# Feed-forward blocks of 384, 384, 384 and 448 columns instead of four of 400, pool weights prepared earlier, sample caches loaded later

## The chip, the core and the metric

The kernel runs on one core of a Trainium2 chip. The metric is device time in microseconds of one execution of the whole program, median of repeated runs. TensorE (PE) multiplies matrices, VectorE (DVE), ScalarE (ACT) and GpSimd (POOL) do the elementwise work, and every transfer is issued by SyncE (SP), whose queue is taken in order.

## The reference, cut to what matters

One layer of a hybrid decoder is applied to a prompt of 2048 tokens and to 8 samples of 8 tokens (64 more columns), all with the same weights, in fp32:

```
h = rmsnorm(x);  proj = h @ w_in                 # 1024 -> 1280: q, k, v and u
attn_o = window attention (128, sinks, ALiBi); samples use cache_win_k, cache_win_v
pool_o = (causal mean over 2, 4, 8, 16 of u - u) @ w_pool * pool_scale; samples use state_pool
x = x + concat(attn_o, pool_o) @ w_out
x = x + cross attention into 256 memory tokens   # samples have their own memory caches
x = x + square(relu(rmsnorm(x) @ w_up)) @ w_down # hidden 4096
y = rmsnorm(x)
```

The outputs are y for both groups and the new window, pool and memory caches.

## The kernel before, in words

Activations lie transposed, features on the 128 partitions and tokens along the free axis. Every fp32 product is made of three fp32r matmuls: an operand is split into a rounded high part and the remainder (`rnd`, and L143 on ACT with L144 on DVE for weights), and high x high, high x low and low x high are added in PSUM (`mm3`, L122 to L124; `dense`, L291 to L293). A weight pair (high, low) is 128x1024 and serves 24 matmuls of a token block.

The prologue computes the memory keys and values, folds them with `w_cq` and `w_co` into matrices that it writes to DRAM (`a_s`, `b_s`), and then three superblocks of two token blocks each follow. The first has 256 and 256 prompt columns, the second block also the 64 sample columns; the other two have 384 and 384. Each superblock goes through the input projection (`in`), attention and pooling (mixed with the rest of the projection), the output projection (`wo`), cross attention, the product with `b_s`, and the feed-forward stage (`up`, `down`): 8 groups of 4 up chunks of 24 matmuls and 4 down pairs of 24 matmuls for each block, so 8 x 4 x 24 + 8 x 4 x 24 = 1536 matmuls per block. In the first superblock the feed-forward runs 512 prompt columns at once. The 64 sample columns leave it before the feed-forward (`xs_s` in DRAM) and ride along in later superblocks: 16 in each of the four blocks, hence 400 columns (`NY`, `NM`).

The weight stream (`Stream`) loads a weight through a staging tile `f` (6 of them), splits it into two of 12 `w` tiles, and runs as many weights ahead as free `w` tiles allow. Small temporaries are `t` tiles (8). The instructions are put on the engines by a scheduler that may move an instruction ahead of others that it does not depend on, but each engine, and SP's queue, runs its list in order.

The pool weights are folded into `w_out`: `prep_fold` loads `cst` and `wpool` and scales `wpool` into a high and low part (L354 on ACT, L355 on DVE), and `fold(g)` multiplies it with the four `wop` weights, between the first chunks of the first superblock's input projection; `put_fold` (L342) copies each result on ACT and writes it to `wo_s`. The loads for the sample part are: `ckz` (1 MB, L534, into the x tile of the second block), `cvz` (two times 512 KB, L522, each in a staging tile `f` until `attn_sample` has ended), `spool`.

Of the kernel before, what the change touches and what calls it, by code (L numbers as in the profile page):

```python
# [9 lines left out]
F32 = mybir.dt.float32  # L10
F32R = mybir.dt.float32r
# [3 lines left out]
P = 128  # L15
# [41 lines left out]
def kernel(ctx: ExitStack, tc: tile.TileContext, io, nW=12, nF=6, nT=8):  # L57
# [13 lines left out]
    FS = Slots([sb(f"f{i}", 1088) for i in range(nF)])  # L71
    ftag = {id(t): f"f{i}" for i, t in enumerate(FS.free)}
    keep = list(FS.free)
    TS = Slots([sb(f"t{i}", 400) for i in range(nT)])
    XT = [sb(f"x{i}", 8 * NM) for i in range(2)]
# [296 lines left out]
    def prologue():  # L372
# [117 lines left out]
    def load_x(bl):  # L490
        src = io["x"][:, 8 * bl.ox:8 * (bl.ox + bl.n)]
        if bl.s == 0:
            nc.sync.dma_start(bl.xt[:, 0:8 * bl.n], src)
        else:
            nc.sync.dma_start(bl.xv[:, :, 0:bl.n], src.rearrange("p (k n) -> p k n", n=bl.n))
            j = 2 * (bl.s - 1) + bl.b
            nc.sync.dma_start(bl.xv[:, :, bl.n:NM], xs_s[:].rearrange("p (k n) -> p k n", n=64)[:, :, 16 * j:16 * j + 16])

    def superblock(s, blks, nxt):
# [15 lines left out]
        if smp:  # L515
            us = X0[:, 4 * uw:4 * uw + 736].rearrange("p (g b t) -> p g b t", g=4, t=23)
            nc.sync.dma_start(X0[:, 4 * uw:4 * uw + 736].rearrange("p (x t) -> p x t", t=23)[:, :, 0:15], io["spool"].rearrange("p (x t) -> p x t", t=15))
            ckz = X1[:, 0:2048].rearrange("p (b v s) -> p b v s", b=8, v=2)
            qz = [X1[:, 2048 + 544 * i:2048 + 544 * (i + 1)] for i in range(2)]
            cvs = [FS.get(), FS.get()]  # L520
            for i in range(2):
                nc.sync.dma_start(cvs[i][:, 0:1024], io["cvz"][:, 1024 * i:1024 * (i + 1)])  # L522
            cvz = [c[:, 0:1024].rearrange("p (b v s) -> p b v s", b=4, v=2) for c in cvs]
            smt = TS.get()
            kS = smt[:, 0:128].rearrange("p (v t) -> p v t", t=64)
            vS = smt[:, 128:384].rearrange("p (v t) -> p v t", t=P)
            nc.gpsimd.memset(smt[:, 0:384], 0.0)
            qf = TS.get()

        def in_evac(c, b, ps):  # L530
            bl = blks[b]
            n = bl.n
            if smp and (c, b) == (0, 0):
                nc.sync.dma_start(X1[:, 0:2048], io["ckz"])  # L534
                nc.gpsimd.memset(X1[:, 2048:3136], 0.0)
            if c == 0:
# [17 lines left out]
                if smp is bl:  # L554
# [207 lines left out]
        def attn_sample():  # L762
            bl = smp
            LS = FS.get()
# [91 lines left out]
        if s == 0:  # L856
            wpr = prep_fold()
        while len(qdone) < len(lead):
# [3 lines left out]
            if s == 0 and m < 4:  # L862
                fold(m, wpr)
# [126 lines left out]
        def sample_cross():  # L990
# [54 lines left out]
            for bg in range(2):  # L1045
                nc.gpsimd.memset(ptz[bg][:, 0:1088], 0.0)
                for mb in range(2):
                    ps = AUX.get()
                    nc.tensor.transpose(ps[:, 0:P], pp[:, 256 * bg + P * mb:256 * bg + P * mb + P], ident[:])
                    for b in range(4):  # L1050
                        nc.vector.tensor_copy(
                            ptz[bg][:, 544 * mb + P * b:544 * mb + P * b + P].rearrange("p (h n) -> p h n", n=32)[:, :, 8 * b:8 * b + 8],
# [5 lines left out]
            for bg in range(2):  # L1058
                for b in range(4):
                    for mb in range(2):  # L1060
                        vv = FS.get()
                        nc.sync.dma_start(vv[:, 0:1024], io["cmv"][4 * bg + b, mb])
                        for h in range(4):
                            nc.tensor.matmul(o2[32 * h:32 * h + 32, 256 * bg:256 * bg + 256],
                                             ptz[bg][:, 544 * mb + P * b + 32 * h:544 * mb + P * b + 32 * h + 32],
# [56 lines left out]
        def after_co(b):  # L1122
# [10 lines left out]
            else:  # L1133
                ml.take += [(GH[b], GH[b].get()) for _ in range(4)]
                if b == 0:
                    ml.f = FS.get()
                    ml.ft = ftag[id(ml.f)]
                    ml.fx = pool.tile([P, 1088], F32R, name=f"{ml.ft}r{s}", tag=ml.ft)
                u = [BIG[f"h{b}"][:, NM * i:NM * i + NM] for i in range(15)] + [ml.fx[:, NM * b:NM * b + NM]]
                ml.h3b[b] = u  # L1140
# [3 lines left out]
        merged = s == 0  # L1144

# [25 lines left out]
        else:  # L1171
            cx = [pool.tile([P, 512], F32R, name=f"cp{b}r{s}", tag=f"cp{b}") for b in range(2)]
            hb = [[BIG[f"q{b}"][:, NM * i:NM * i + NM] for i in range(15)] + [cx[b][:, 0:NM]] for b in range(2)]
            hidu = lambda b, g, i: hb[b][8 * (g % 2) + i]
# [94 lines left out]
        if not merged:  # L1269
            FS.ids.discard(id(ml.f))  # L1270
            f = pool.tile([P, 1088], F32, name=f"{ml.ft}f{s}", tag=ml.ft)
            ftag[id(f)] = ml.ft
            keep.append(f)
            FS.ids.add(id(f))
            FS.put(f)
# [8 lines left out]
    vcarry = [None]  # L1284
    blk = [make_blks(s) for s in range(3)]
# [134 lines left out]
```

## Time and profile before

| what | us |
|---|---|
| median of 3 runs (lowest, highest) | 2657.72 (2656.19, 2660.29) |
| the profiled execution | 2660.15 |
| its span, first to last instruction | 2658.3 |
| PE busy | 2576.7 (97%) |
| DVE, ACT, POOL busy | 1298.3, 974.8, 658.9 |
| prologue | 0 to about 117 |
| input projection of the first superblock up to its sample attention | about 117 to 177 |
| feed-forward of the three superblocks | about 467 to 830, 1168 to 1745, 2074 to 2646 |

The span is what the trace covers; the time of the execution holds 1.85 us more. PE's busy share is not its speed: what counts is the distance between the starts of matmuls and the stretches in which PE waits. The second half of a clock column, PEclk, tells the share of full speed that PE was granted.

### The profile page before, as it was taken

To read this page: it belongs to the slowest core of one execution; us is meant where nothing else is said; L and a number is where in the kernel's file an instruction comes from. 1 tells how busy PE (TensorE), PEld (TensorE's weight loads), DVE (VectorE), ACT (ScalarE), POOL (GpSimd) and SP (SyncE) were. 2 spreads that over 40 slices of the span, in tenths; PEclk is the share of its full clock that TensorE was granted. 3 is DMA by queue.
4 is the path that set the end of the run, shared out by engine and by line. 5 is a ranking of instruction groups with operands and counts; after the bars stand their busy time and mean duration, and the time that the engine had idled before them with its cause. 6 is when DMAs were issued, how large, how long until landed. Compare 5 with 4: busy or idle time off the path is not lost.

```text
span 2658.3 us, 36411 instructions
## 1 busy us (share of the span) xinstructions
PE 2576.7 (97%) x14409; PEld 2407.6 (91%) x14409; DVE 1298.3 (49%) x2256; ACT 974.8 (37%) x1867; POOL 658.9 (25%) x695
## 2 busy tenths in 40 slices
PE   8789999999999999999999999999999999999998
PEld 8688858888879998899999999999979999999997
DVE  7547634644447856353333333689363633333333
ACT  6536424422334744333222222358243422222221
POOL 1205312311125343142111111525332411111111
PEclk9989999999999999999999999999999999999999
DMA  8842266223233041212111111222211111111101
GB/s 275 265 149 89 104 238 237 79 93 104 95 102 128 25 145 33 74 45 72 64 56 64 56 64 56 81 107 81 97 48 64 56 64 64 56 64 56 64 24 50
DMA packets 101823, 245.10 MB, mean 92 GB/s; under 512 B 21972, under 2 KB 41876, under 8 KB 101012
## 3 DMA queue, kind: packets, MB, share of 16 engines
q1 hardware_dynamic: 101652, 242.78, 26.9%
q8 instruction: 113, 1.85, 0.3%
q14 instruction: 58, 0.48, 0.1%
HBM read 219.79 MB, written 22.95 MB: 91 GB/s over the span
## 4 chain that ended last, share of the span: by engine, by line
PE 80%; DVE 8%; ACT 4%; POOL 3%; DMA 3%; issue 2%; SPq 0%; DVEq 0%; ACTq 0%; POOLq 0%
PE mm L124 13%; PE mm L122 13%; PE mm L123 13%; PE mm L292 13%; PE mm L293 12%; PE mm L291 12%; DVE t L243 3%; DVE w L144 1%; POOL t L217 1%; ACT w L143 1%; PE aux L699 1%; DVE acth L246 1%; POOL t L617 1%; ACT x L711 1%; PE aux L730 1%
## 5 line engine op out<-in xcount | busy, mean ns | idle before, releaser
L143 ACT CAST w<-f 128x1024 fp32r<-128x1024 f32 x311 | 325.9, 1050 | 693.3 <-PE mm L123 470.0
L144 DVE TENSOR_TENSOR w<-f,w 128x1024 fp32r<-128x1024 f32 x311 | 393.3, 1269 | 302.8 <-ACT w L143 298.4
L291 PE MATMUL mm<-acth,w 128*128 128x400 f32 (+3 forms) x1568 | 532.6, 340 | 6.6 <-ACT w L143 5.9
L293 PE MATMUL mm<-acth,w 128*128 128x400 f32 (+3 forms) x1568 | 529.4, 338 | 1.2 <-DVE w L144 1.2
L292 PE MATMUL mm<-acth,w 128*128 128x400 f32 (+3 forms) x1440 | 486.8, 338 | 6.1 <-DVE acth L246 5.4
L122 PE MATMUL mm<-actq,w 128*128 128x400 f32 (+2 forms) x1376 | 478.2, 348 | 1.1 <-ACT f L342 1.1
L124 PE MATMUL mm<-actq,w 128*128 128x400 f32 (+2 forms) x1376 | 478.7, 348 | 0.0
L123 PE MATMUL mm<-actq,w 128*128 128x400 f32 (+2 forms) x1248 | 433.5, 347 | 0.0
L1178 POOL TENSOR_TENSOR t<-t 128x400 f32<-128x400 f32 (+1 forms) x136 | 163.1, 1200 | 812.3 <-ACT t L1177 812.3
L291 PEld LDWEIGHTS mm<-acth,w 128*128 128x128 f32 x1568 | 298.1, 190 | 10.1 <-ACT w L143 6.8
L293 PEld LDWEIGHTS mm<-acth,w 128*128 128x128 f32 x1568 | 299.2, 191 | 1.7 <-DVE w L144 1.7
L1239 DVE TENSOR_TENSOR x<-mm,x 128x400 f32<-128x400 f32 (+1 forms) x272 | 152.9, 564 | 281.6 <-PE mm L124 278.6
L292 PEld LDWEIGHTS mm<-acth,w 128*128 128x128 f32 x1440 | 273.9, 190 | 11.2 <-DVE acth L246 7.3
L217 POOL TENSOR_TENSOR t<-t,t 128x384 f32<-128x384 f32 (+3 forms) x161 | 191.2, 1188 | 351.7 <-ACT t L216 348.3
L122 PEld LDWEIGHTS mm<-actq,w 128*128 128x128 f32 x1376 | 259.5, 189 | 11.7 <-ACT f L342 1.5
L124 PEld LDWEIGHTS mm<-actq,w 128*128 128x128 f32 x1376 | 260.8, 190 | 9.5
L291 PE MATMUL mm<-actq,w 128*128 128x384 f32 (+2 forms) x768 | 248.0, 323 | 0.8 <-DVE x L915 0.6
L293 PE MATMUL mm<-actq,w 128*128 128x384 f32 (+2 forms) x768 | 246.2, 321 | 2.0 <-DVE w L144 2.0
L292 PE MATMUL mm<-actq,w 128*128 128x384 f32 (+2 forms) x768 | 246.5, 321 | 0.0
L123 PEld LDWEIGHTS mm<-actq,w 128*128 128x128 f32 x1248 | 235.4, 189 | 9.9
L1180 DVE TENSOR_TENSOR actq<-t,actq 128x400 fp32r<-128x400 f32 (+1 forms) x120 | 71.1, 593 | 222.1 <-ACT actq L1179 222.0
L291 PEld LDWEIGHTS mm<-actq,w 128*128 128x128 f32 x768 | 145.6, 190 | 3.3 <-DVE x L915 0.9
(246 smaller groups left out, 3745.3 us busy)
## 6 DMA issues: line engine op xcount, KB each, us to landing
f<-in_wup SPq DMA_DIRECT2D x89, 512.0 KB, 3.2
f<-in_wdn SPq DMA_DIRECT2D x89, 512.0 KB, 3.2
f<-in_win SPq DMA_DIRECT2D x29, 512.0 KB, 3.2
f<-a_s SPq DMA_DIRECT2D x23, 512.0 KB, 3.8
f<-b_s SPq DMA_DIRECT2D x23, 512.0 KB, 4.2
f<-in_wco SPq DMA_DIRECT2D x16, 512.0 KB, 4.9
f<-in_cmk SPq DMA_DIRECT2D x16, 512.0 KB, 4.2
f<-in_cmv SPq DMA_DIRECT2D x16, 512.0 KB, 5.1
```

Of the source, the lines that this page charges most:

```text
L122: nc.tensor.matmul(ps, Wh(k), Hh(k), start=first and i == 0, stop=False)
L123: nc.tensor.matmul(ps, Wh(k), Hl(k), start=False, stop=False)
L124: nc.tensor.matmul(ps, Wl(k), Hh(k), start=False, stop=final and i == last)
L143: nc.scalar.copy(th[:], r[:, 0:1024])
L144: eng.tensor_tensor(tl[:], r[:, 0:1024], f32(th[:]), ALU.subtract)
L217: self.add.tensor_tensor(self.acc[:, 0:n], self.acc[:, 0:n], t[:, 0:n], ALU.add)
L243: nc.vector.scalar_tensor_tensor(t[:, 0:n], self.x(k), vec[:, g + k:g + k + 1], self.r[:, 0:n], ALU.mult, ALU.mult)
L291: nc.tensor.matmul(ps[:, 0:n], w8(th)[:, k, :], hi(b, k), start=k == 0, stop=False)
L292: nc.tensor.matmul(ps[:, 0:n], w8(th)[:, k, :], lo(b, k), start=False, stop=False)
L293: nc.tensor.matmul(ps[:, 0:n], w8(tl)[:, k, :], hi(b, k), start=False, stop=k == 7)
L1178: nc.gpsimd.tensor_tensor(q, r, r, ALU.mult)
L1239: nc.vector.tensor_tensor(bl.x(m), ps[:, 0:n], bl.x(m), ALU.add)
```

## The change

1. **Widths.** All 64 sample columns ride in the last block: `NX` and `NY` become 384, 384, 384 for the first three blocks of superblocks two and three, and 448 for the last. A block of 384 columns finds its 16 operands in its own activation tiles (`units`); the block of 448 columns fits 13 there and takes 3 (of the up stage) from two staging tiles `f`, and 1 plus 2 (of the down stage) from `f` and `cp` tiles. So superblock two holds back no `f` tile in its feed-forward (one before), and superblock three two (one before). The x loads of the blocks without sample columns become one contiguous run per partition, and the four loads of 16 columns from `xs_s` become one of 64.
2. **Tiles.** `t` tiles are 448 columns wide and 7 instead of 8; `f` tiles 1024 instead of 1088.
3. **Pool weights.** `prep_fold` is called in the prologue, at the fourth chunk of the fold with `w_cq`, instead of at the input projection.
4. **Sample caches.** In program order `ckz` is loaded at chunk 2 of the input projection instead of chunk 0, `cvz` and `spool` at chunk 4 instead of ahead of the projection, and the copy of the old window keys to `out_wks` is issued in `attn_sample`.

```diff
-OFFY = [0, 256, 512, 912, 1312, 1712]
-NX = [256, 320, 400, 400, 400, 400]
-NY = [256, 256, 400, 400, 400, 400]
-NM = 400
+OFFY = [0, 256, 512, 896, 1280, 1664]
+NX = [256, 320, 384, 384, 384, 448]
+NY = [256, 256, 384, 384, 384, 448]
...
-def tile_hybrid_step_kernel(ctx: ExitStack, tc: tile.TileContext, io, nW=12, nF=6, nT=8):
+def tile_hybrid_step_kernel(ctx: ExitStack, tc: tile.TileContext, io, nW=12, nF=6, nT=7):
...
-    FS = Slots([sb(f"f{i}", 1088) for i in range(nF)])
+    FS = Slots([sb(f"f{i}", 1024) for i in range(nF)])
...
-    TS = Slots([sb(f"t{i}", 400) for i in range(nT)])
+    TS = Slots([sb(f"t{i}", 448) for i in range(nT)])
...
         for c in range(8):
+            if c == 3:
+                wpr.append(prep_fold())
             th, tl = S.next(("cq", c))
...
-            j = 2 * (bl.s - 1) + bl.b
-            nc.sync.dma_start(bl.xv[:, :, bl.n:NM], xs_s[:].rearrange("p (k n) -> p k n", n=64)[:, :, 16 * j:16 * j + 16])
+            if bl.nx > bl.n:
+                nc.sync.dma_start(bl.xv[:, :, bl.n:bl.nx], xs_s[:].rearrange("p (k n) -> p k n", n=64))
...
-            if smp and (c, b) == (0, 0):
+            if smp and (c, b) == (2, 0):
                 nc.sync.dma_start(X1[:, 0:2048], io["ckz"])
                 nc.gpsimd.memset(X1[:, 2048:3136], 0.0)
+            if smp and (c, b) == (4, 1):
+                for i in range(2):
+                    cvs.append(FS.get())
+                    nc.sync.dma_start(cvs[i][:, 0:1024], io["cvz"][:, 1024 * i:1024 * (i + 1)])
+                    cvz.append(cvs[i][:, 0:1024].rearrange("p (b v s) -> p b v s", b=4, v=2))
+                nc.sync.dma_start(X0[:, 4 * uw:4 * uw + 736].rearrange("p (x t) -> p x t", t=23)[:, :, 0:15], io["spool"].rearrange("p (x t) -> p x t", t=15))
...
-                        nc.sync.dma_start(io["wks"][r, :, 0:120], ckz[r, :, kv, 8:P])
...
-        if s == 0:
-            wpr = prep_fold()
...
-                fold(m, wpr)
+                fold(m, wpr[0])
...
-                if b == 0:
-                    ml.f = FS.get()
-                u = [BIG[f"h{b}"][:, NM * i:NM * i + NM] for i in range(15)] + [ml.fx[:, NM * b:NM * b + NM]]
+                if bl.ny > NB:
+                    ml.f = [FS.get() for _ in range(2)]
+                    ml.ex = [x[:, bl.ny * i:bl.ny * i + bl.ny] for x in ml.fx for i in range(2)]
+                ml.h3b[b] = u = units("h", bl, 0, 3)
...
+        def units(g, bl, a, z, more=()):
+            n = bl.ny
+            u = [BIG[f"{g}{bl.b}"][:, n * i:n * i + n] for i in range(16 * NB // n)]
+            if n > NB:
+                u += ml.ex[a:z] + list(more)
+            return u
```

The lists of the engines move at three places. The first is SP's queue behind the last group of `b_s` writes, where the input projection begins (`win` and `wop` are weights, `wo_s` the folded results). Before:

```order
L522 DMA f_82<-in_cvz 128x1024
L522 DMA f_81<-in_cvz 128x1024
L351 DMA f_83<-in_wpool 128x512
L561 DMA out_wks<-x_94 512x1x120
L557 DMA out_wks<-t_92 1024x1x8
L561 DMA out_wks<-x_94 512x1x120
L344 DMA wo_s<-f_84 128x4x128
L344 DMA wo_s<-f_79 128x4x128
L142 DMA f_83<-in_win 128x1024
L142 DMA f_84<-in_wop 128x1024
```

In the changed kernel:

```order
L530 DMA x_93<-in_ckz 128x2048
L342 DMA wo_s<-f_82 128x4x128
L342 DMA wo_s<-f_83 128x4x128
L140 DMA f_84<-in_win 128x1024
L140 DMA f_79<-in_wop 128x1024
L559 DMA out_wks<-t_89 1024x1x8
L342 DMA wo_s<-f_80 128x4x128
L342 DMA wo_s<-f_82 128x4x128
L140 DMA f_83<-in_wop 128x1024
L140 DMA f_80<-in_win 128x1024
L140 DMA f_82<-in_win 128x1024
L767 DMA out_wks<-x_93 512x1x120
```

`cvz` and `wpool` are gone from here, `ckz` has come (before, it stood 24 rows further up, ahead of the last `a_s` write), and the second `win` weight still stands behind the two `wo_s` writes of the first fold.

The second place is SP's queue where the fold with `w_cq` writes its first results (`a_s`). In the changed kernel, with `wpool` ahead of the first `a_s` write and the last `wcqt` weight behind the fifth, where it stood ahead of the first:

```order
L398 DMA out_mv<-t_86 128x256
L349 DMA f_84<-in_wpool 128x512
L342 DMA a_s<-f_82 128x512
L342 DMA a_s<-f_83 128x512
L342 DMA a_s<-f_79 128x512
L342 DMA a_s<-f_80 128x512
L342 DMA a_s<-f_82 128x512
L140 DMA f_79<-in_wcqt 128x1024
```

The third is PE's list after the first chunk of the input projection. Before, the second block's part of that chunk (128x320) came first and the fold (128x512) after all of it:

```order
L292 MATMUL mm_98<-acth_64,w_71 128x320
L293 MATMUL mm_98<-acth_64,w_72 128x320
L122 MATMUL mm_96<-w_73,w_69 128x512
L123 MATMUL mm_96<-w_74,w_69 128x512
L124 MATMUL mm_96<-w_73,w_69 128x512
L122 MATMUL mm_97<-w_73,w_69 128x512
```

In the changed kernel the first fold stands ahead of the second block's part:

```order
L290 MATMUL mm_94<-acth_63,w_73 128x256
L291 MATMUL mm_94<-acth_63,w_74 128x256
L120 MATMUL mm_95<-w_75,w_77 128x512
L120 MATMUL mm_96<-w_75,w_77 128x512
L289 MATMUL mm_97<-acth_64,w_73 128x320
L121 MATMUL mm_95<-w_76,w_77 128x512
```

The fold has moved by one chunk of 24 matmuls on PE. The lines of the changed kernel have numbers lower by 2 here: the copy L342 is L340, its write L344 is L342, `dense`'s L291 to L293 are L289 to L291.

More of the change, by code (lines that the diff above doesn't have):

```diff
@@ L56, with kernel @@
 @with_exitstack
[L57 removed]
+def kernel(ctx: ExitStack, tc: tile.TileContext, io, nW=12, nF=6, nT=7):
     nc = tc.nc
@@ L763, in attn_sample @@
             bl = smp
+            for kv in range(2):
+                r = slice(64 * kv, 64 * kv + 64)
+                nc.sync.dma_start(io["wks"][r, :, 0:120], ckz[r, :, kv, 8:P])
             LS = FS.get()
@@ L1171, in superblock, with hidb @@
         else:
-            cx = [pool.tile([P, 512], F32R, name=f"cp{b}r{s}", tag=f"cp{b}") for b in range(2)]
-            hb = [[BIG[f"q{b}"][:, NM * i:NM * i + NM] for i in range(15)] + [cx[b][:, 0:NM]] for b in range(2)]
-            hidu = lambda b, g, i: hb[b][8 * (g % 2) + i]
+            hb = {}
+            def hidb(b):
+                if b not in hb:
+                    more = []
+                    if blks[b].ny > NB:
+                        more = [pool.tile([P, 512], F32R, name=f"cp{i}r", tag=f"cp{i}")[:, 0:blks[b].ny] for i in range(2)]
+                    hb[b] = units("q", blks[b], 3, 4, more)
+                return hb[b]
+            hidu = lambda b, g, i: hidb(b)[8 * (g % 2) + i]
         def relu2(ps, hi, lo, n, r, q):
```

28 lines of the change are left out of this document (8 added, 20 removed).

## The prediction

> **What bounds the kernel now.** I read the engines' shares and the chain of waits first.
>
> ```profile
> PE 2576.7 (97%) x14409; PEld 2407.6 (91%) x14409; DVE 1298.3 (49%) x2256; ACT 974.8 (37%) x1867; POOL 658.9 (25%) x695
> PE 80%; DVE 8%; ACT 4%; POOL 3%; DMA 3%; issue 2%; SPq 0%; DVEq 0%; ACTq 0%; POOLq 0%
> ```
>
> PE sets the end nearly everywhere, so two things can move the time: the distance between matmul starts in the long stages, and the stretches in which PE waits or runs slowly. For the first, matmuls counted in stretches of one width, two of feed-forward and one of the prologue (window, PE busy and count, weight loads, DVE, ACT, POOL, then PEclk and DMA), and DVE's adds behind groups of 24 matmuls at 384 columns, two groups apart:
>
> ```profile
> 1300.00:1700.00 400.00, 400.00 (x2196) 399.73 (x2195) 145.46 (x200) 102.76 (x160) 74.00 (x65) 1.00 0.19 64
> 30.00:58.00 28.00, 28.00 (x234) 27.95 (x233) 23.87 (x37) 16.55 (x29) 7.81 (x9) 1.00 0.89 299
> 500.00:760.00 260.00, 260.00 (x1149) 215.36 (x1148) 111.52 (x169) 77.31 (x96) 38.16 (x24) 1.00 0.28 98
> ...
> 2057.07 0.56 DVE L1119 TENSOR_TENSOR x<-mm,x 128x384 f32<-128x384 f32 x1 [3.60 <-PE mm L293]
> 2065.39 0.56 DVE L1119 TENSOR_TENSOR x<-mm,x 128x384 f32<-128x384 f32 x1 [3.60 <-PE mm L293]
> ```
>
> At 400 columns a matmul starts every 400.00 / 2196 = 0.1821 us; at 512 columns (first superblock) every 260.00 / 1149 = 0.2263; at 256 (prologue) every 28.00 / 234 = 0.1197; at 384 every 8.32 / 48 = 0.1733. PE never waits there, at full clock. The line through 384 and 512 has 0.0530 / 128 = 0.00041 us per column; at 256 it gives 0.1208, near the 0.1197, at 400 it gives 0.1799. So 400 columns lie 2.2 ns above the line.
>
> For the second, the place where PE loses most, the start of the first input projection:
>
> ```profile
> 100.00:120.00 20.00, 17.68 (x81) 14.24 (x81) 5.82 (x5) 11.69 (x18) 0.00 (x0) 0.91 0.97 299
> 120.00:140.00 20.00, 8.71 (x36) 6.95 (x34) 6.27 (x15) 7.30 (x17) 1.60 (x6) 0.74 0.76 215
> 140.00:160.00 20.00, 16.31 (x79) 14.87 (x80) 7.61 (x10) 8.16 (x11) 0.00 (x0) 0.76 0.72 219
> ...
> L291 PE MATMUL mm<-acth,w 128*128 128x320 f32 x21 | 7.1, 337 | 1.8 <-ACT w L143 1.8
> L291 PE MATMUL mm<-acth,w 128*128 128x256 f32 x10 | 4.3, 432 | 4.1 <-ACT w L143 4.1
> L122 PE MATMUL mm<-w,w 128*128 128x512 f32 x8 | 4.2, 531 | 7.9 <-ACT w L354 7.9
> ```
>
> The last three rows are the groups of 120 to 160 us with the wait ahead of each behind the second bar. L292 and L293 go with L291, L123 and L124 with L122, so PE ran 63 matmuls of 320 columns, 30 of 256 and 24 of 512. By the line these take 63 x 0.147 + 30 x 0.121 + 24 x 0.226 = 18.3 us, and 40 went by: 21.7 lost. Waits are 7.9 + 4.1 + 1.8 = 13.8 of it; most of the rest is the clock, granted at 0.74 and 0.76. The chain of waits, in order of time, tells what was late:
>
> ```profile
> 115.61 6.28 DMA f<-in_wop
> 121.91 1.06 ACT w L143
> 123.00 1.24 DVE w L144
> 124.69 6.12 DMA f<-in_wpool
> 135.45 4.17 DMA f<-in_win
> 139.65 1.05 ACT w L143
> ```
>
> The pool weights were issued at 124.69, behind 1 MB of `cvz`; the fold waited for them. The next `win` weight was issued at 135.45 only, since it stands behind the fold's two writes on SP.
>
> **Feed-forward widths.** Nothing is added or removed: 1536 matmuls per block before and after, 1600 columns in four blocks. Before, four blocks cost 4 x 0.1821 = 0.7284 us per matmul of each. After, 3 x 0.1733 plus a matmul of 448 columns, which the trace does not have. Bounds: on the line, 0.1733 + 64 x 0.00041 = 0.1998; with twice the 2.2 ns that 400 columns lie above it, 0.2042. I take the line: 256, 384 and 512 columns all start their operands at multiples of 256 bytes and lie on it, and operands of 448 columns (1792 bytes) do so too, where those of 400 columns (1600 bytes) do not; that this is the cause is my inference. The gain is (0.7284 - 0.5199 - 0.1998) x 1536 = **13.4**, with the other bound 6.6.
>
> The elementwise work of a 448-column chunk stays hidden: one up chunk takes PE 24 x 0.1998 = 4.8 us, and its slowest step is POOL's square,
>
> ```profile
> L1178 POOL TENSOR_TENSOR t<-t 128x400 f32<-128x400 f32 (+1 forms) x136 | 163.1, 1200 | 812.3 <-ACT t L1177 812.3
> SPq L142 <- DVE w L144: 1800.3, 246, 30.9
> ```
>
> 1.2 us at 400, 1.35 at 448. With seven `t` tiles three chunks of two are in flight, 14 us of PE time; uncovered, a wait of 1.2 us on each of 128 chunks would cost 154. In the last superblock the weight stream has four staging tiles instead of five; the second row (waits of SP: total, times, longest) says that SP already waits for staging tiles, but up to five finished weight pairs stand ahead of PE, 8.7 us each. I cost both at 0.
>
> The Trainium skill, "TensorE: Matmul & The Clock Gate", section "Back-to-back issue gap", gives the isolated gap as N/2.4 + 2.5 ns: 169.2 at 400, 162.5 at 384. By it the four blocks need the same time before and after, and the term would be 0, since it knows only a sum of columns. The rows differ from it by 10.8 ns at 384 and 12.9 at 400, so the measurement decides for an offset that depends on the width.
>
> **Start of the input projection.** The load of `wpool`, four scalings on ACT and four on DVE move some 60 us forward, two loads of `cvz` some 20 us later, and `ckz` goes from 93 us to just behind the last `b_s` write. The fold then waits for its own `wop` and for nothing else. What is late next is the second `win`: on SP it stays behind the fold's two writes, and 1 MB of `ckz` now goes ahead of it.
>
> ```profile
> 130.89 1.28 ACT L354 ACTIVATE w<-f,vec 128x128 fp32r<-128x128 f32 x4 [2.74 <-DMA f<-in_wpool]
> ...
> 133.07 0.59 ACT L342 COPY f<-mm 128x512 f32<-128x512 f32 x1 [0.91 <-ACT w L354]
> ...
> 131.32 1.23 DVE L355 SCALAR_TENSOR_TENSOR w<-f,vec,w 128x128 fp32r<-128x128 f32 x4 [2.46 <-ACT w L354]
> ...
> f<-wo_s SPq DMA_DIRECT2D x22, 256.0 KB, 2.9
> ```
>
> From the fold's first copy (133.07) to the end of the `win` cast (140.7) went 7.6 us. In the changed order PE has for it half a fold, the second block's chunk and the second fold: 0.7 + 24 x 0.147 + 6 x 0.226 = 5.6, so a wait of 2.0 stays. `ckz` can add between 0 and 3.2, the difference between 6.12 (`wpool` behind 1 MB) and 2.9 (256 KB alone, last row); I take half, 3.5 in all, and 0.8 for the low part on DVE. The wait for `wop`, needed now at 119.7, is at most 121.91 + 1.06 - 119.7 = 3.3; at 299 GB/s the missing 1 MB brings it 3.5 us forward; I take 1. For the clock after such pauses I take 3 of the 7 or so lost before. Left are 8.3 of 21.7: gain **13**. Ends: all waits at their upper ends, another 1.8 for the third weight, and the clock loss unchanged leave 18 lost, gain 4; only 2.0 + 0.8 lost, gain 19.
>
> `cvz` lands some 10 us of query chunks ahead of the sample attention; its `out_wvs` copies hold SP until then, and behind them stand weights of the eighth chunk and later, for which PE has the sample attention to do. I cost it at 0; uncovered, one landing, about 4.
>
> On the clock the same page of the Trainium skill, section "The HAM clock gate", says that about 3.4 us of idling puts PE at half rate until about 3.4 us of work have passed. The rows agree (a wait of 7.9 us, PEclk 0.74). If no pause after the change reaches 3.4, the gain would by that rule be 3 larger.
>
> **Prologue.** One wait on the path stands behind `ckz`:
>
> ```profile
> 100.28 4.23 DMA f<-in_wco
> 104.53 1.05 ACT w L143
> ```
>
> Without the 1 MB, this load comes earlier, up to 3.5. Against it the scalings (1.28 on ACT, 1.23 on DVE, rows above) and one staging tile enter a stretch where staging tiles turn over at once, and the last `wcqt` goes behind five writes: up to 4 (one landing). I take a gain of **1**.
>
> **Small ends.** The 448-column block's norm is 12% longer. Its last sum is where PE already waits (start, duration):
>
> ```profile
> 2080.00 1.21 POOL L246 TENSOR_TENSOR f4r<-t,acth 128x400 fp32r<-128x400 f32 x1 [1.07 <-ACT acth L244]
> 2081.17 2.01 POOL L217 TENSOR_TENSOR t<-t,t 128x400 f32<-128x400 f32 x1
> 2098.07 1.37 POOL L246 TENSOR_TENSOR f4r<-t,acth 128x400 fp32r<-128x400 f32 x1
> ...
> x<-in_x SPq DMA_DIRECT2D x4, 1536.0 KB, 7.1
> PE mm L291 <- DVE x L915: 0.6, 1, 0.6
> ...
> 2650.53 4.46 DVE L1256 SCALAR_TENSOR_TENSOR x<-x,vec,t 128x400 f32<-128x400 f32 x8
> ```
>
> The sum at 2081.17 grows by 0.24, and the 17 us from there to the last operand at 2099.4 by about 1.3, while PE arrives 96 x 0.0088 = 0.8 sooner: a loss of **1.5**, between 0.5 and 4. The x loads, one run per partition instead of eight, are worth at most the 0.6 that PE waits for one; the tail on the last block, now 384 columns, shortens 4% of about 9 us, 0.4; the norms of the other two blocks 0.3: together a gain of **1.2**.
>
> **Sum.** 13.4 + 13 + 1 - 1.5 + 1.2 = 27.1. The profiled execution took 2660.15 (span 2658.3 and 1.85 around it): 2633.0. It lies 2.4 above the median of the runs; from the median it would be 2630.6. I forecast **2633**.
>
> **Rivals.**
> - *Only the sum of columns counts*, or the excess at 400 is traffic of the other engines that stays: gain 13.7, 2646. For it: DVE, ACT and POOL work all through the feed-forward. Against it: they do so at 512 columns too, and 256, 384 and 512 lie on one line. The gap rule of the Trainium skill is of this kind. Chance 0.10.
> - *The stall only moves*: the second `win` behind `ckz` takes the place of the pool weights, gain 4 instead of 13: 2642. For it: SP's order, and DMA busy 0.97 at 100 to 120. Against it: the fold itself starts earlier. Chance 0.14.
> - *Four staging tiles bound the last feed-forward*: its 64 weights arrive late. From 27.1 / 64 = 0.42 us per weight the whole gain is gone; one landing of 3.2 us in every fourth costs 51, 2684, slower. For it: SP's waits above. Against it: the weight pairs in reserve. Chance 0.04.
> - That the change does nothing is excluded by the widths and the moved rows; a gain lost to several small waits, no difference: 0.02.
>
> The forecast has 0.70. **Range**: best 13.4 + 19 + 3.5 + 1 = 37, 2623; worst of the likeliest 6.6 + 4 - 3 - 2.8 + 1 = 6, 2654, which needs all at once; 2622 to 2647 covers the first two rivals' times and leaves the rest out. A measurement of this kernel tells 0.2%, 5.3 us, from no change. The first three cases end faster, less 0.02 for their own slack: faster 0.92, same 0.04, slower 0.04.
>
> **What would show it.** Right: DVE's adds in the feed-forward come every 12 x 0.1733 = 2.08 us for three blocks and 2.40 for the last; the wait for the scaled pool weights is gone, PE's longest wait between 117 and 160 us is under 5, and PEclk there is over 0.85; the `win` cast, not `wpool`, is what PE waits for. Wrong: 448 columns at 0.204 or more; a wait of 6 us or more for `win`; waits of PE for weights after 2100 us.

## The result, and the profile after

The changed kernel takes 2640.03 us (median of 4 runs, 2638.20 to 2640.77) against 2657.77 (4 runs, 2656.19 to 2660.29) for the one before: ratio 0.9931, 95% interval 0.9914 to 0.9949, a gain of 17.7 us. Forecast were 2633 and a range of 2622 to 2647, so the time lies in the range and 7 us above the forecast. The profiled execution took 2638.20 (span 2636.4), 21.95 less than the profiled one of before. The engines' shares:

```profile
PE 2563.7 (97%) x14409; PEld 2367.3 (90%) x14409; DVE 1296.8 (49%) x2256; ACT 973.8 (37%) x1867; POOL 652.9 (25%) x695
```

PE still sets the end, with the same 14409 matmuls, so the start of the n-th can be compared between the two traces. That tells where the 21.95 us came from:

| from matmul to matmul | what runs there | before, us | after, us | gain | forecast |
|---|---|---|---|---|---|
| start to 700 | prologue | 115.5 | 117.2 | -1.7 | +1 |
| 700 to 950 | first input projection | 59.5 | 44.6 | +14.9 | +13 |
| 950 to 3000 | rest of superblock one up to its feed-forward | 318.2 | 312.3 | +5.9 | 0 |
| 3000 to 6600 | its feed-forward, superblock two up to feed-forward | 718.3 | 714.8 | +3.5 | see below |
| 6600 to 9000 | feed-forward of superblock two | 437.2 | 416.0 | +21.2 | see below |
| 9000 to 11400 | superblock three up to feed-forward | 445.8 | 444.1 | +1.7 | see below |
| 11400 to 14400 | feed-forward of superblock three | 548.8 | 573.3 | -24.5 | see below |
| 14400 to the end | last norm, and the 1.8 us outside the span | 17.0 | 16.0 | +1.0 | see below |

The last five rows are the widths with their small ends, forecast at 13.4 - 1.5 + 1.2 = 13.1 in all; they brought 2.9. Even that is not all theirs: in the row from 3000 to 6600 the kernel before has 10.2 us in which the trace grants PE half its clock, the changed one 3.4, and that difference alone is worth 3.4 of the row's 3.5 us. The runs further down with widths of 400 have 715.8 to 720.9 us in this row, more where more of it ran at half rate. The start of the projection and the stretch behind it brought more than forecast. Two windows of 400 us in the feed-forward of superblocks two and three, and the three windows at the start of the projection (columns as in the prediction):

```profile
100.00:120.00 20.00, 17.18 (x66) 13.13 (x65) 4.81 (x4) 10.09 (x16) 0.00 (x0) 0.83 0.87 256
120.00:140.00 20.00, 16.03 (x84) 14.24 (x83) 9.85 (x15) 10.20 (x18) 1.63 (x6) 0.83 0.95 307
140.00:160.00 20.00, 20.00 (x140) 19.74 (x139) 11.80 (x21) 10.43 (x16) 0.00 (x0) 1.00 0.87 251
1200.00:1600.00 400.00, 400.00 (x2310) 400.00 (x2309) 137.92 (x193) 96.67 (x145) 53.80 (x48) 1.00 0.18 63
2100.00:2500.00 400.00, 400.00 (x2109) 380.73 (x2108) 132.81 (x179) 88.76 (x130) 49.63 (x43) 1.00 0.17 58
```

At 384 columns a matmul starts every 400.00 / 2310 = 0.1732 us, as forecast. Blocks of 384 and 448 in turn give 400.00 / 2109 = 0.18967 on the mean, so a matmul of 448 columns takes 2 x 0.18967 - 0.1733 = 0.2060, where the forecast took 0.1998. DVE's adds in the last feed-forward (start, duration), one behind every 12 matmuls of the `down` stage, show it directly:

```profile
2201.21 0.56 DVE L1256 TENSOR_TENSOR x<-mm,x 128x384 f32<-128x384 f32 x1
2203.29 0.56 DVE L1256 TENSOR_TENSOR x<-mm,x 128x384 f32<-128x384 f32 x1 [1.52 <-PE mm L122]
2205.76 0.62 DVE L1256 TENSOR_TENSOR x<-mm,x 128x448 f32<-128x448 f32 x1 [1.91 <-PE mm L122]
2208.21 0.62 DVE L1256 TENSOR_TENSOR x<-mm,x 128x448 f32<-128x448 f32 x1 [1.82 <-PE mm L122]
...
2210.29 0.56 DVE L1256 TENSOR_TENSOR x<-mm,x 128x384 f32<-128x384 f32 x1
```

Twelve matmuls of 384 take 2.08 us, twelve of 448 take 2.47 and 2.45. The prediction wanted 2.40, and had named 0.204 or more per matmul as what would prove it wrong.

PE's waits between 117 and 160 us (total, times, longest), the two longest kinds:

```profile
PE mm L289 <- ACT w L141: 3.3, 1, 3.3
PE mm L120 <- DVE w L546: 0.7, 1, 0.7
```

The wait of 7.9 us for the scaled pool weights is gone. What is late is the second `win` weight, as the prediction said. SP's queue (start, duration) shows why:

```profile
120.58 1.73 SPq L530 DMA_DIRECT2D x<-in_ckz  x1
125.08 0.91 SPq L342 DMA_DIRECT2D wo_s<-f  x2
126.04 0.62 SPq L140 DMA_DIRECT2D f<-in_win  x1
```

The weight is issued at 126.04, behind the two writes of the fold and the 1 MB of `ckz`; the cast of it on ACT starts at 131.04, 5 us later.

### The profile page after: what moved, and what is told of

Read it like the earlier page. It is cut to its first block, busy times and chain, and to the rows that moved or that the text cites. A ratio compares the mean times of both kernels' runs of the same rounds, so it can differ in the third digit from the quotient of the medians.

```text
span 2636.4 us, 36430 instructions
## 1 busy us (share of the span) xinstructions
PE 2563.7 (97%) x14409; PEld 2367.3 (90%) x14409; DVE 1296.8 (49%) x2256; ACT 973.8 (37%) x1867; POOL 652.9 (25%) x695
## 5 line engine op out<-in xcount | busy, mean ns | idle before, releaser
L141 ACT CAST w<-f 128x1024 fp32r<-128x1024 f32 x330 | 345.7, 1051 | 759.4 <-PE mm L121 506.0
L142 DVE TENSOR_TENSOR w<-f,w 128x1024 fp32r<-128x1024 f32 x330 | 418.8, 1274 | 324.1 <-ACT w L141 318.9
L289 PE MATMUL mm<-acth,w 128*128 128x384 f32 (+3 forms) x1568 | 531.0, 339 | 5.3 <-ACT w L141 3.3
L291 PE MATMUL mm<-acth,w 128*128 128x384 f32 (+3 forms) x1568 | 527.0, 336 | 0.0
L290 PE MATMUL mm<-acth,w 128*128 128x384 f32 (+3 forms) x1472 | 492.9, 335 | 5.5 <-DVE acth L244 4.9
L120 PE MATMUL mm<-actq,w 128*128 128x384 f32 (+3 forms) x1376 | 477.5, 347 | 1.6 <-ACT f L340 1.6
L122 PE MATMUL mm<-actq,w 128*128 128x384 f32 (+3 forms) x1376 | 475.9, 346 | 0.0
L121 PE MATMUL mm<-actq,w 128*128 128x384 f32 (+3 forms) x1280 | 439.4, 343 | 0.0
L1195 POOL TENSOR_TENSOR t<-t 128x384 f32<-128x384 f32 (+2 forms) x136 | 158.3, 1164 | 817.0 <-ACT t L1194 814.7
L289 PEld LDWEIGHTS mm<-acth,w 128*128 128x128 f32 x1568 | 297.5, 190 | 13.5 <-ACT w L141 3.7
L291 PEld LDWEIGHTS mm<-acth,w 128*128 128x128 f32 x1568 | 297.2, 190 | 5.2 <-DVE w L142 0.3
L1256 DVE TENSOR_TENSOR x<-mm,x 128x384 f32<-128x384 f32 (+2 forms) x272 | 152.6, 564 | 277.5 <-PE mm L122 277.2
L120 PEld LDWEIGHTS mm<-actq,w 128*128 128x128 f32 x1376 | 259.6, 189 | 17.1 <-ACT f L340 2.0
L289 PE MATMUL mm<-actq,w 128*128 128x384 f32 (+2 forms) x768 | 247.2, 322 | 0.7 <-ACT w L141 0.4
L291 PE MATMUL mm<-actq,w 128*128 128x384 f32 (+2 forms) x768 | 245.5, 320 | 1.2 <-DVE w L142 1.2
L1197 DVE TENSOR_TENSOR actq<-t,actq 128x384 fp32r<-128x384 f32 (+2 forms) x124 | 71.3, 575 | 222.3 <-ACT actq L1196 222.3
L289 PEld LDWEIGHTS mm<-actq,w 128*128 128x128 f32 x768 | 144.9, 189 | 3.1 <-ACT w L141 0.9
```

Source lines behind the costliest of these rows:

```text
L120: nc.tensor.matmul(ps, Wh(k), Hh(k), start=first and i == 0, stop=False)
L121: nc.tensor.matmul(ps, Wh(k), Hl(k), start=False, stop=False)
L122: nc.tensor.matmul(ps, Wl(k), Hh(k), start=False, stop=final and i == last)
L141: nc.scalar.copy(th[:], r[:, 0:1024])
L142: eng.tensor_tensor(tl[:], r[:, 0:1024], f32(th[:]), ALU.subtract)
L289: nc.tensor.matmul(ps[:, 0:n], w8(th)[:, k, :], hi(b, k), start=k == 0, stop=False)
```

## The experiments

The leading theory was that the widths brought little because 448 columns have a price of their own, and that the start of the projection gained because SP's queue ahead of the second `win` weight became shorter. Each part was done alone, matmuls were timed alone, and the two were then corrected or split further. The ratios are each to runs of the kernel before on the same chip (medians 2659.19, 2659.64 and 2658.84 in the three groups of runs).

**Matmuls alone.** Ninety-six fp32r matmuls per arrangement, with nothing else running beside them but one small copy on DVE behind each 24. An arrangement is a number of columns `n`, a distance from operand to operand `stride`, and a first start `off`:

```diff
+    def cfg(f, n, stride, off=0, po=0, groups=4):
+        h = lambda k: H[:, off + stride * k:off + stride * k + n]
...
+            for k in range(8):
+                f(q, w(wh, k), h(k), start=k == 0, stop=False)
+                f(q, w(wh, k), h(8 + k), start=False, stop=False)
+                f(q, w(wl, k), h(k), start=False, stop=k == 7)
```

> Measures the disputed cost by itself: the layer is left out, PE runs 31 groups of 96 matmuls (the three products of a split fp32 product, 8 operands high and low) at one width each, with the operands at a given distance in SBUF, and nothing but one small copy per 24 matmuls runs beside it; the outputs are not computed. In the changed kernel a 448-column matmul starts every 0.206 us, where the line through 384 and 512 gives 0.200, and a 400-column one 0.182 where it gives 0.180. Theory A, the operands' distance or start: at a distance of 512 columns 448 comes to 0.200 and 400 to 0.180, at 448 and 400 they come to 0.206 and 0.182. Theory B, the width itself: 448 costs 0.206 at every distance. Theory C, traffic of the other engines: both lie on the line at every distance.

None of the three theories holds as it was put. DVE's copies (start, duration, and in brackets the line of the matmul group that released them), first and last of four groups, so 72 matmuls apart. L86 is 400 columns at a distance of 512 from operand to operand, L89 448 at 512, L96 the same with all starts 16 columns further, L98 64 columns further, L100 400 at 400, L105 384 at 400:

```profile
125.36 0.17 DVE L126 COPY o<-mm 128x16 f32<-128x16 f32 x1 [4.14 <-PE mm L86]
138.32 0.18 DVE L126 COPY o<-mm 128x16 f32<-128x16 f32 x1 [4.14 <-PE mm L86]
...
180.06 0.17 DVE L126 COPY o<-mm 128x16 f32<-128x16 f32 x1 [4.70 <-PE mm L89]
194.65 0.17 DVE L126 COPY o<-mm 128x16 f32<-128x16 f32 x1 [4.69 <-PE mm L89]
...
322.21 0.17 DVE L126 COPY o<-mm 128x16 f32<-128x16 f32 x1 [4.63 <-PE mm L96]
336.62 0.17 DVE L126 COPY o<-mm 128x16 f32<-128x16 f32 x1 [4.63 <-PE mm L96]
...
361.15 0.17 DVE L126 COPY o<-mm 128x16 f32<-128x16 f32 x1 [4.78 <-PE mm L98]
376.03 0.17 DVE L126 COPY o<-mm 128x16 f32<-128x16 f32 x1 [4.79 <-PE mm L98]
...
400.24 0.17 DVE L126 COPY o<-mm 128x16 f32<-128x16 f32 x1 [4.20 <-PE mm L100]
413.36 0.17 DVE L126 COPY o<-mm 128x16 f32<-128x16 f32 x1 [4.20 <-PE mm L100]
...
486.07 0.17 DVE L126 COPY o<-mm 128x16 f32<-128x16 f32 x1 [4.03 <-PE mm L105]
498.75 0.17 DVE L126 COPY o<-mm 128x16 f32<-128x16 f32 x1 [4.05 <-PE mm L105]
```

Divided by 72: 400 columns take 180.0 ns at a distance of 512 and 182.2 at 400; 384 columns take 176.1 at a distance of 400 (and 173.3 at 384, 448 and 512). So the 2.2 ns of the kernel before belong to the distance from operand to operand, and the prediction was right that they go when operands start at multiples of 64 columns. But 448 columns take 202.6 there, and 206.7 with starts 64 columns further, and only 200.1, the line, with starts 16 columns further. The operands' position thus decides in both cases, but the position that is best for 400 columns is not best for 448. Beside PE only DVE's small copies run here, so the excess is not the other engines' traffic.

**The widths alone**, pool weights and caches as before:

```diff
-NX = [256, 320, 400, 400, 400, 400]
+NX = [256, 320, 384, 384, 384, 448]
```

> Before, with the widths, the tiles and the x loads of the change, and the pool weights and caches as before. The traces of before and after give, per matmul of each of four blocks, 4 x 0.1820 = 0.7280 before and 3 x 0.1734 + 0.2058 = 0.7260 after, so 3 us in 1536; the starts of the norms and x loads may add 1. Theory 1 (widths worth next to nothing, the gain is all at the start): 2653 to 2657, ratio 0.998 to 1.000. Rival (the widths are worth the 13 of the prediction, and something else lost it): 2645, ratio 0.995.

Measured: 2655.16, ratio 0.9984 (0.9975 to 0.9993). The widths are worth some 4 us of the 17.7, not 13.

**Pool weights and caches alone**, widths of 400; the last row stands for the loads of `cvz` and `spool`:

```diff
+            if c == 3:
+                wpr.append(prep_fold())
...
-            if smp and (c, b) == (0, 0):
+            if smp and (c, b) == (2, 0):
...
+            if smp and (c, b) == (4, 1):
```

> Before, with the pool weights prepared in the prologue and the sample caches loaded later, and 400 columns as before. Theory 1: it takes the change's time to within 3 us, 2640 to 2644, ratio 0.993 to 0.995. Rival: the widths carry the gain, 2645 to 2650, ratio 0.995 to 0.997.

Measured: 2642.36, ratio 0.9935 (0.9921 to 0.9948). Nearly the whole gain of the change is here. The two gains, 4.0 and 16.8, add up to 20.8, the change gives 17.7; with intervals of 2 to 5 us to either side that is no proof of a loss, but the traces have one: at matmul 700 both parts alone are ahead of before (111.5 and 112.7 us against 115.5), together they are behind (117.2).

**Pool weights alone**, caches as before:

```diff
+            if c == 3:
+                wpr.append(prep_fold())
...
-        if s == 0:
-            wpr = prep_fold()
```

> Before, with the pool weights prepared in the prologue alone; caches and widths as before. If the pool weights were the whole stall, the gain of the start (about 17 us) stays: 2641 to 2643. If the caches' place in SP's queue matters as much (cvz still ahead of the second win weight, two staging tiles held, ckz still ahead of the wco weight), half of it: 2647 to 2652. Theory of the prediction: the second win weight then waits behind 1 MB of cvz, as long as it would behind ckz, so about 2643.

Measured: 2657.36, ratio 0.9998 (0.9989 to 1.0007): nothing, where each of the three expectations had a gain, though the wait for the pool weights is gone here too. The window of 120 to 140 us and, below it, the chain of waits of this run:

```profile
120.00:140.00 20.00, 4.68 (x23) 3.43 (x22) 5.08 (x12) 6.66 (x13) 1.61 (x6) 0.64 0.87 244
```

```profile
120.98 9.35 DMA x<-in_ckz
...
130.39 0.57 SPq L563
...
131.68 5.73 DMA f<-in_win
...
137.43 1.05 ACT w L143
```

PE ran 23 matmuls in 20 us. It waited 13.1 us for the second `win` weight, which SP issued at 131.68, since two copies to `out_wks` (L563) stood ahead of it, and SP held them until the `ckz` that they read had landed, 9.35 us after its issue behind 1 MB of `cvz`; for the landing itself SP stood 2.0 us. This is the rival "the stall only moves", with another last link than the one it named: a store in SP's list that waits for a load.

**The store moved too**: pool weights early, and the `out_wks` copy issued in `attn_sample`:

```diff
-                        nc.sync.dma_start(io["wks"][r, :, 0:120], ckz[r, :, kv, 8:P])
...
+                nc.sync.dma_start(io["wks"][r, :, 0:120], ckz[r, :, kv, 8:P])
```

> Before, with the pool weights prepared early and the copy of the old window keys to out_wks issued in the sample attention; cvz and ckz loads, widths as before. With the pool weights alone PE waited 13.3 us for the second win weight, which on SP stood behind that copy, which waited 9.4 us for ckz behind cvz. If SP's wait for ckz was the cause, the gain of the start returns: 2643 to 2648. If the 2 MB of cvz and ckz ahead of the weight are the cause, it does not: 2652 to 2658.

Measured: 2655.05, ratio 0.9986 (0.9976 to 0.9995), as forecast for the case that the 2 MB matter. The longest wait for the weight falls from 13.1 to 9.0 us: the store was a part of it. The weight is issued at 127.07 now, and 2 MB of `cvz` and `ckz` are still ahead of it in the transfer.

**Caches alone**, with the store moved, pool weights as before:

```diff
+            cvs, cvz = [], []
...
-            if smp and (c, b) == (0, 0):
+            if smp and (c, b) == (2, 0):
```

> Before, with the sample caches and the out_wks copies later, and the pool weights prepared at the input projection as before. If the early pool weights are needed as well, the fold still waits for wpool, now without 1 MB of cvz ahead of it: 3 to 6 us shorter, 2651 to 2656. If the caches alone carry the gain: 2642.

Measured: 2651.54, ratio 0.9968 (0.9956 to 0.9979). The fold still waits for its pool weights, 4.8 us instead of 7.9, and the weight behind it 1.2.

**One cache at a time**, with the pool weights early and the store moved. First `cvz` and `spool` later, `ckz` as before; then `ckz` later, `cvz` as before (the condition of the first, then that of the second):

```diff
+            if smp and (c, b) == (4, 1):
...
-            if smp and (c, b) == (0, 0):
+            if smp and (c, b) == (2, 0):
```

> The kernel before with the pool weights prepared early, the out_wks copy issued in attn_sample, and cvz and spool loaded at the fifth chunk; ckz stays at chunk 0 and the widths stay at 400. Theory V (what is ahead of the second win weight and shares the transfer with it is cvz, and its two staging tiles are held until the sample attention): the longest wait of PE for that weight falls from the 9.2 us of the run with cvz in its old place to 3 to 5, and the time is that of the run with all sample caches moved, 2642 to 2646 (ratio 0.993 to 0.9955). Theory K (any 1 MB less of the two would do, and with ckz in its old place the weight still waits): the wait stays at 6 or more and the time is 2650 to 2655.

> The same with the other cache moved: ckz at chunk 2, cvz and spool ahead of the projection as before. Theory V: the weight still waits 7 us or more behind cvz, time 2650 to 2655 (ratio about 0.998). Theory K: 1 MB less in either place is enough, wait under 5 and 2643 to 2647 (ratio 0.994 to 0.996).

Measured: 2646.1, ratio 0.9953 (0.9936 to 0.9969), and 2649.14, ratio 0.9967 (0.9954 to 0.9980). PE's waits for weights between 117 and 160 us, of the first run and of the second:

```profile
PE mm L291 <- ACT w L143: 5.1, 1, 5.1
```

```profile
PE mm L291 <- ACT w L143: 7.5, 2, 4.2
```

Neither theory holds as it was put. Theory V forecast 7 us or more where only `ckz` moves, and there were 4.2; theory K forecast 6 or more where only `cvz` moves, and there were 5.1. By the times alone both runs lie within 1 us of what theory V gave. What both runs have in common is 1 MB ahead of the weight instead of 2, and its wait is then 4 to 5 us whichever it is. The second run has a further wait of 3.3 us. SP's queue of it shows what held the weight back:

```profile
128.66 0.67 SPq L536 DMA_DIRECT2D x<-in_ckz  x1
131.88 0.38 SPq L344 DMA_DIRECT2D wo_s<-f  x1
132.65 0.33 SPq L142 DMA_DIRECT2D f<-in_wop  x1
136.90 0.58 SPq L767 DMA_DIRECT2D out_wks<-x  x1
137.53 1.58 SPq L344 DMA_DIRECT2D wo_s<-f  x2
141.26 0.82 SPq L142 DMA_DIRECT2D f<-in_win  x2
```

SP stood before `out_wks` for 3.9 us until `ckz` had landed, then 2.0 us more for a staging tile, and the next `win` weights came at 141.26. It is the same store behind the same load, later in the program; how much of the 3.3 us is due to it is not shown, since no run moved it further. The intervals of the two runs overlap, so which cache counts more stays open.

**Where the 448-column operands start.** Matmuls alone again, 29 arrangements, most of 448 columns, some with the weights starting `wo` columns further:

```diff
-        w = lambda t, k: t[:, P * k:P * k + P]
+        w = lambda t, k: t[:, wo + P * k:wo + P * k + P]
```

> The layer left out as in the first measurement of widths; now mostly 448 columns at a distance of 448, with the first operand 0 to 80 columns into its tile, some widths around it, and the weights 16 or 64 columns into theirs. There, 448 cost 0.2027 with starts at 0, 0.2000 with all starts 16 columns on (distance 512), 0.2039 at 32 and 0.2067 at 64 and 128. Theory A (start within 64 columns decides): 0.200 at 16 and 80 for a distance of 448 too, over 0.202 at 0 and 64. Rival D (what decides is the phase in which PE happens to be, not the operands): repeats of the same layout differ among themselves as much as layouts do, and moving the weights by 16 columns changes as much as moving the operands.

Measured, ns per matmul by first start, with weights starting at multiples of 64 columns:

| start | 0 | 4 | 8 | 12 | 16 | 20 | 24 | 28 | 32 | 40 | 48 | 56 | 64 | 80 |
|---|---|---|---|---|---|---|---|---|---|---|---|---|---|---|
| ns | 202.6 | 202.2 | 206.7 | 203.0 | 200.0 | 203.3 | 205.4 | 206.7 | 203.9 | 200.0 | 202.2 | 204.4 | 206.7 | 200.0 |

With the weights 16 columns further too, a start of 16 gives 206.7 instead of 200.0. With the operands at 0 and the weights 16, 32 or 48 columns further (the latter two in the run below) it is 202.2, 204.0 and 200.0, the values of the starts 48, 32 and 16. So what counts is where the operand starts against where the weights start, modulo 64 columns, and 16, 40 and 80 lie on the line: theory A. The starts 0 and 16, repeated at the end of the run, gave 202.7 and 200.1.

> Matmuls alone, the layer is left out; 96 fp32r matmuls of 448 columns per start of the operands, at multiples of 32 and 64 columns from the tile's start, with the weights at multiples of 16 to 64 and PSUM at 0, 32 and 64. Theory S (operand start less weight start, modulo 64 columns, sets the pitch): all multiples of 64 agree with one another, at 202.7 or 206.7 ns, and 32 lies at 204 with weights at 0 and at 202 to 207 with weights at 32. Rival M (the modulus is 128 columns or more): starts at 64, 192 and 320 give 206.7 and starts at 0, 128 and 256 give 202.7. Rival O (what came before sets it, not the start): the values at multiples of 64 differ without order.

A third run of matmuls alone asked for the modulus. All eleven arrangements with starts at multiples of 64 columns took 202.6 to 202.7 ns, all six with starts at odd multiples of 32 took 203.9 to 204.0. Groups 72 matmuls apart as above, of a start at 64 columns, in this run and, in the second fence, in the run before:

```profile
94.12 0.17 DVE L125 COPY o<-mm 128x16 f32<-128x16 f32 x1 [4.70 <-PE mm L84]
...
108.71 0.18 DVE L125 COPY o<-mm 128x16 f32<-128x16 f32 x1 [4.69 <-PE mm L84]
```

```profile
290.93 0.17 DVE L125 COPY o<-mm 128x16 f32<-128x16 f32 x1 [4.79 <-PE mm L94]
...
305.80 0.17 DVE L125 COPY o<-mm 128x16 f32<-128x16 f32 x1 [4.78 <-PE mm L94]
```

That is 14.59 / 72 = 202.6 and 14.87 / 72 = 206.5 ns for one and the same arrangement (the rows' two digits leave 0.1 to 0.2 ns open). Theory S holds in that starts 64 columns apart agree within this run, and the modulus of 128 falls. But the position alone doesn't set the value, and rival O is not excluded for that: the two runs were on different chips, and a start of 56 columns ran before in the one, of 32 in the other. Which of these matters, or whether something else does, isn't shown. Which of the two values the kernel gets (its mean is 0.2060, near the upper) can't be told from the layout.

**The changed kernel with the 448-column operands 16 columns further in:**

```diff
-            u = [BIG[f"{g}{bl.b}"][:, n * i:n * i + n] for i in range(16 * NB // n)]
+            o = 16 if n > NB else 0
+            u = [BIG[f"{g}{bl.b}"][:, o + n * i:o + n * i + n] for i in range((16 * NB - o) // n)]
```

The tiles `ml.ex` and `cp` start at column 16 likewise.

> The changed kernel, with the sixteen operands of the 448-column block 16 columns further into their tiles. Theory A: 448 columns start every 0.200 instead of 0.206 in the last feed-forward, 1536 x 0.0058 = 9 us less: 2631, ratio to before 0.990. Rival D: no difference to the changed kernel, 2640, ratio 0.993.

Measured: 2631.91 (2629.88 to 2633.57), ratio to the kernel before 0.9900 (0.9885 to 0.9914). The window of the last feed-forward:

```profile
2100.00:2500.00 400.00, 400.00 (x2141) 386.21 (x2140) 135.80 (x182) 89.92 (x131) 49.67 (x43) 1.00 0.18 60
```

The mean is 0.18683, so 448 columns take 0.2004. The 1536 matmuls of 448 columns save 0.2060 - 0.2004 = 0.0056 each, 8.6 us; the two medians differ by 8.1, and by 10.0 where each is taken against its own runs of before. This version beats both kernels.

**The widths alone with that start:**

```diff
-NX = [256, 320, 400, 400, 400, 400]
+NX = [256, 320, 384, 384, 384, 448]
...
+            o = 16 if n > NB else 0
```

> Widths 384, 384, 384 and 448 alone, everything else as before, with the 448-column operands 16 columns further in. If the first term of the prediction failed by the price of a 448-column matmul alone (0.2058 measured, 0.1998 taken), its operands starting 16 columns further in (0.2003) bring back 1536 x 0.0055 = 8.4 us from the widths alone: 2655.2 - 8.4 = 2646.8, ratio 0.9952 (0.993 to 0.9965). If something else ate the gain of the widths (tiles, staging), it stays within 3 us of the widths alone: 2653 to 2656.

Measured: 2647.43, ratio 0.9956 (0.9941 to 0.9971), a gain of 11.4 against 4.0 for the widths alone with the old start; 0.6 from the expectation. With operands on the line the widths bring what the prediction wanted of them, 13.4 for the feed-forward less 0.3 for its two small terms, within the interval.

## Why the prediction was right and wrong, step by step

**Feed-forward widths: wrong, and this is the step that failed.** The term of 13.4 took 0.1998 us for 448 columns, the lower of its two bounds. The reason given was that operands of 448 columns start at multiples of 256 bytes, as those of 256, 384 and 512 do, and those of 400 don't. The runs confirm the half on 400 columns and refute the half on 448: at such starts they take 0.2026 to 0.2067. By the measured 0.2060 the term is (0.7284 - 0.5199 - 0.2060) x 1536 = 3.8, below even the pessimistic bound of 6.6, which doubled the excess at 400 (2.2 ns) where the real one is 6. The bound was drawn from one row, though nothing said that the excess grows no faster. With the corrected start the widths alone gain 7.4 us more than without it.

**Elementwise work and staging tiles: right.** In the last feed-forward PE is busy 400.00 of 400 us in the window above, at full clock; no wait for weights appears after 2100. The rival of four staging tiles falls.

**Start of the projection: right in size, not in its reason.** 14.9 us gained where 13 were forecast; the second `win` is what is late, 3.3 us where 3.5 was taken for ACT's part, and PEclk is 0.83 and 1.00 where 0.74 and 0.76 stood. The fold's wait for `wop` is gone, where 1 us was taken. The clock still lost about what was taken, 3. Of the changed kernel's trace, two stretches (columns as above; PEclk is the 0.50):

```profile
104.32:111.14 6.82, 6.35 (x14) 4.69 (x15) 2.43 (x2) 3.14 (x5) 0.00 (x0) 0.50 0.93 247
131.62:138.45 6.83, 6.31 (x27) 5.98 (x28) 2.45 (x2) 2.05 (x3) 0.34 (x2) 0.50 0.85 233
```

In the second, behind the wait of 3.3 us, PE is busy for 6.31 us at half rate, which costs it half of that. In the first, in the prologue, a wait of 2.4 us is enough. The Trainium skill ("TensorE: Matmul & The Clock Gate", "The HAM clock gate") names about 3.4 us of idling for the fall to half rate. Here shorter waits were followed by it, and so the 3 us that the prediction would add by that rule did not come. What the prediction told too simply is why: it credited the pool weights, and noted the cache loads for what they would cost. The pool weights alone are worth nothing (0.9998), the caches and the store alone 0.9968, both 0.9935. The caches and the store alone bring half of the gain; the whole needs both, because the two reasons for the stall stand one behind the other: take away the first, and PE stops 13.1 us for the second. The prediction's own rival, that the stall only moves, is what happens without the cache moves.

**What came unforeseen behind it: 5.9 us** between matmuls 950 and 3000. The kernel before has 318.2 us there in its profiled execution; the six runs with widths of 400 and some of the other edits have 315.2 to 317.6, the two with the new widths alone 314.2 and 315.4, and the changed kernel 312.3. Most of it is the granted clock: from 177 to 300 us and from 300 to 467 it was 0.94 and 0.99 before, 0.97 and 1.00 after. By the trace's own clock records that is 17.1 us at half rate between these matmuls before and 6.8 after, and the difference is worth up to 5.1 us. What sets these stretches off wasn't traced to an edit.

**Prologue: wrong in sign, -1.7 for +1.** In the window of 100 to 120 us PE ran 66 matmuls at a clock of 0.83, against 81 at 0.91: half rate for 6.8 us in the changed kernel, as shown above, and for 3.4 us in the one before, behind a wait of 2.2 us. The 3.4 us more are worth about the 1.7 that the row lost. Up to matmul 700 the four kernels with early pool weights beside the old widths and old or half-moved caches gain 2.1 to 5.6, pool weights and all caches 2.8, and the widths alone (with their 7 `t` tiles) 4.0. The caches and the store alone lose 0.8; the change and its version with the new starts lose 1.7 and 0.5. The first four and the widths alone have no half rate ahead of 120 us. So the widths and the pool weights help here and the loss belongs to the combination. PE's wait of 2.4 us there is for a weight; why it comes late in the combination wasn't tried and stays open.

**Small ends: right.** The stretch with the 448-column norm, matmuls 10800 to 11400, lies 1.6 us further above its matmuls' own time than before; 1.5 was taken.

**The rivals.** "Only the sum of columns counts" gave 2646 and 0 us for the widths in the feed-forward; the widths' 3.8 comes near to that, but not for its reason: the excess at 400 columns does go, and one at 448 takes its place. With the start 16 columns further in the sum of columns is the same and the time 8 us lower, so the rule falls. Of this kind is the rule of the Trainium skill, "TensorE: Matmul & The Clock Gate", section "Back-to-back issue gap": N/2.4 + 2.5 ns, for the isolated gap, has no term for the operand's position; at 400 columns it gives 169.2, and the runs show 180.0 and 182.2.

The sum of the terms by measurement is -1.7 + 14.9 + 5.9 + 2.9 = 22.0 against 27.1. So the terms were 5 us off together: the widths were 10 and the prologue 2.7 too high, and two others, 8 together, too low, most of it a difference in the clock that the prediction does not have. The other 2 us up to the 7 by the medians are that the profiled execution lies 1.8 under the median of the changed kernel. That the time fell into the range is therefore in part luck: it held by these cancelling as well as by its width.

## What to carry to other kernels

The time of a stream of fp32r matmuls isn't a function of the column count alone: before a width is chosen, time the widths with the very operand starts that the kernel will use, since 16 columns of offset were worth 8 us here. Of a stall, list everything that stands ahead of the late transfer in the issuing queue, the stores that wait for loads too, because taking away the first cause only shows the second. An inference from three points that lie on a line is worth a range at the fourth, not a point.

## What the runs showed of the hardware

- Back to back and with nothing else running, fp32r matmuls of 256, 320, 352, 384, 496 and 512 columns start every 120.0, 146.7, 160.0, 173.3, 220.0 and 226.7 ns with operands at multiples of 512 columns, all on N/2.4 + 13.3. Widths between lie off it at those starts: 288 takes 131.7 (1.6 below), 416 188.3, 432 195.8, 448 202.7, 464 210.0, 480 216.7 (1.7 to 3.3 above).
- The excess moves with the start of the operand against the start of the weights: 448 columns take 200.0 at 16, 40 and 80 columns and up to 206.7 elsewhere. 512 columns, on the line at distance 512, take 228.9 with starts 16 columns further: an offset that helps one width costs at another.
- Two values, 202.7 and 206.7, occur for the same arrangement in different runs. Why stays open.
- Waits of PE of 2.2, 2.4 and 3.3 us were each followed by 3.4 to 6.8 us at half the clock. The difference in such stretches alone accounts for 1.7, up to 5.1 and 3.4 us of the first, third and fourth row of the table.
